# One decoder trunk on one core: compression ahead of d's second pair, other homes for four tiles, and another form of softplus

## Chip, cores and metric

The kernel runs on one core of a Trainium2 chip. The metric is the device time of one execution in microseconds (us); the median of three runs stands for the kernel.

## The reference, cut to what matters

Two layers over 512 tokens of width 1024. In each layer four attention branches read the same normalised input h, each result is gated, projected and merged:

```python
for l in range(DEPTH):                      # DEPTH = 2
    h = rmsnorm(x, norm_g[l])
    c = split_columns(h @ w_in[l])          # columns a_*, b_*, c_*, d_*
    y_a = dilated_window_attention(...) * silu(c["a_gate"])
    y_b = mla_attention(...)            * silu(c["b_gate"])
    y_c = nsa_attention(...)            * silu(c["c_gate"])   # uses compress_blocks
    y_d = stick_breaking_attention(...) * silu(c["d_gate"])
    for i, y in enumerate((y_a, y_b, y_c, y_d)):
        merged += sigmoid(h @ w_merge[l, i] + b_merge[l, i]) * (y @ w_branch[l, i])
    x = x + merged @ w_out[l]
```

Branch d (stick breaking) needs softplus(z) = log(1 + exp(z)) of its scores z, summed from the right, and exp(z - that sum). Compression (`compress_blocks`, for c's first part) takes overlapping blocks of 32 tokens of two 64-wide columns, adds a position table, multiplies by w1 (2048 x 128 for each of the two), applies gelu and multiplies by w2.

## The kernel before, in words

Every product of 1024-long columns is made in three matmuls of a high and a low half (`mm3`, lines 188 to 190), 128 x 128 by 128 x 512. Such a product of one 128-column chunk of weights with all tokens is a **chunk**: its weights come by DMA on the queue of SyncE (SP) into one of 3 `stage` buffers (line 239), ScalarE (L182), GpSimd (L100) and VectorE (L184) split them into halves (4 `w5` tiles, so two chunks), and TensorE runs 24 matmuls (`proj_T`). A chunk of `merge_chunks` has 6 more for the branch (`pd<-y,w`). Chunks need only h (and a y in the merge), so they are the filler between the small matmuls of attention.

An attention pair (two heads) runs the steps scores on TensorE (`qk_unit`, L290, into one of 2 `pss` banks), softmax on VectorE and ScalarE (L300 to L307), transposes (L325, `pt`), a copy on ScalarE (L327) and the product with v (L331, into the one bank `po`). `pv_cluster` holds the last three. Each layer has 30 clusters (6 in b, 6 in a, 6 in d, 12 in c). Branch order is b, a, d, c. In d the scores z go to `ze[0]` (L740), then L742 takes min(z, 30) on VectorE into `ze[1]`, L743 its exponential, L746 log(1 + that) on ScalarE, and L748 takes the larger of z and that on VectorE; prefix sums (L756), a difference (L757) and an exponential (L758) follow. `after(...)` on line 751 orders L748 of two tiles behind the splits of two later weight chunks.

A scheduler orders the instructions of each engine: it takes what is ready by priority, which is the place in the program. `tc.high_priority(offset)` moves a block ahead by `offset` places; the four attention branches are moved ahead of the chunks that stand beside them in the program. Each engine then executes its list in order; a DMA queue too.

Tiles share slots by tag: `s4` has 11, `x4` 4, `y4` 8, PSUM `pd` 3. A new tile waits until a slot is free. Names in what follows:

- b's stage: chunks for b's gate, d's q and k (both pairs) and a's gate, beside b's attention, whose q and k tiles are `x4`.
- a's stage: the two table tiles `tab_a` (`x4`, line 692), a's q and k (`y4`), merge (0, 1), d's gate, then `compress()`, then merge (1, 0).
- `compress()`: chunk c_kc, 8 additions on VectorE (L609) that form the blocks, a chunk for ks and kw (split at L175 and L176 into two `s4` tiles), four w1 tiles of 512 KB (`s4`, DMA of line 626), 16 small matmuls for each (L629).
- d's `ze` tiles are `x4` (four for a pair) and unit tiles.

The functions that the diff touches, with the line numbers of the profile:

Of the kernel before, what the change touches and what calls it, by code (L numbers as in the profile page):

```python
# [12 lines left out]
AF = mybir.ActivationFunctionType  # L13
OP = mybir.AluOpType
PSUM = bass.MemoryType.PSUM

P = 128
# [28 lines left out]
W_SHARE = 5  # L46

PV_GROUPS = ((0, 1), (2,), (3,))
N_S4, N_W5, N_TH, N_PT, N_SU, N_S2 = 11, 4, 2, 4, 5, 4

MERGE_REST = ((2, 0), (2, 1), (2, 3), (3, 0), (3, 3), (0, 3), (3, 1), (1, 3), (0, 2), (1, 2), (2, 2), (3, 2))
# [35 lines left out]
def hybrid_trunk(ctx: ExitStack, tc: tile.TileContext, x, norm_g, w_in, mla_q_norm, mla_w_uq, mla_kv_norm,  # L87
                 mla_w_ukv, nsa_pos, nsa_w1, nsa_b1, nsa_w2, nsa_b2, w_branch, w_merge, b_merge, w_out,
                 final_norm_g, tab_a_d, mask_tab_d, dist_tab_d, cmp_tab_d, rope_tab_d, small_d, out):
    nc = tc.nc  # L90
    V, A, G, T = nc.vector, nc.scalar, nc.gpsimd, nc.tensor
# [16 lines left out]
    def s4(shape, dt=F32):  # L108
        return mk(sb, shape, dt, "s4", N_S4)
# [4 lines left out]
    def x4(shape, dt=F32):  # L114
        return mk(sb, shape, dt, "x4", 4)
# [22 lines left out]
    def ps_d():  # L138
        return mk(ps, [P, 512], F32, "pd", 3)
# [170 lines left out]
    def after(first, then, why):  # L310

        tc.add_manual_dep(then.ins, first.ins.name, mybir.DependencyInfo(
            mybir.DependencyClass.Sync, mybir.DependencyReason.DATA), reason=why)

    def pv_cluster(units, acc):

        blocks = [(u, kb) for u in units for kb in range(u[1] + 1)]
        n = len(blocks)  # L320
        pTs = []
        for h in range(2):
            pt = ps_t().rearrange("p (a q) -> p a q", a=4)
            for i, (u, kb) in enumerate(blocks):
                T.transpose(pt[:, i], u[0][h][:, kb * P:(kb + 1) * P], ident)  # L325
            pT = pt_tile()
            ready = A.activation(pT[:, :n], pt[:, :n], AF.Copy)  # L327
            pTs.append(pT)
        for i, ((_, qt, v, started, last), kb) in enumerate(blocks):
            for h in range(2):  # L330
                pv = T.matmul(acc[64 * h:64 * h + 64, qt * P:(qt + 1) * P], v(h, kb), pTs[h][:, i],  # L331
                              start=(kb == 0 and not started), stop=(kb == qt and last), skip_group_check=True)
                if kb == 0:
                    after(ready, pv, "both heads together")

    def finish_pair(acc, g, y, c):

# [73 lines left out]
    for t in range(NT):  # L411
        x_in.append(x4([P, D]))
        for c0 in range(0, D, 512 if t == 0 else D):
            c = slice(c0, c0 + (512 if t == 0 else D))
# [28 lines left out]
    for l in range(DEPTH):  # L443
# [140 lines left out]
        def compress():  # L584
            b1 = tiny([P, 2], "b1", 1)
            nc.sync.dma_start(b1, nsa_b1[l].rearrange("s p -> p s"))
            b2k = tiny([P, 1], "b2k", 1)
            for hf in range(2):
                nc.sync.dma_start(b2k[64 * hf:64 * hf + 64], nsa_b2[l, 0].rearrange("(d o) -> d o", o=1))
            b2v = tiny([P, 64], "b2v", 1)  # L590
            nc.sync.dma_start(b2v, bcast_rows(nsa_b2[l, 1], 64))
            w2k = tiny([P, 2, 64], "w2k", 1)
            w2v = tiny([P, 64], "w2v", 1)
            for hf in range(2):
                nc.sync.dma_start(w2k[:, hf], nsa_w2[l, 0])
            nc.sync.dma_start(w2v, nsa_w2[l, 1])

            acc = ps_d()
            proj_T(in_chunk(l, COL["c_kc"]), acc)
            blocks = []  # L600
            for s_ in range(2):
                sm = s2([P, 16, 32])
                V.memset(sm[:, :, NCMP:], 0.0)
                tokv = acc[64 * s_:64 * s_ + 64].rearrange("p (n q r) -> p r q n", r=2, q=8)
                for r in range(2):
                    for qh in range(2):
                        src = tokv[:, r, :, qh:qh + NCMP]
                        pos = posT[l][64 * r:64 * r + 64, 16 * s_ + 8 * qh:16 * s_ + 8 * qh + 8, None]
                        V.tensor_tensor(sm[64 * r:64 * r + 64, 8 * qh:8 * qh + 8, :NCMP], src,  # L609
                                        pos.to_broadcast([64, 8, NCMP]), op=OP.add)  # L610
                blocks.append(sm)
            acc = ps_d()
            proj_T(split_chunk([(0, KD, 0, 64, wview(w_in[l], 0, D, COL["c_ks"], 64)),
                                (0, KD, 64, 128, wview(w_in[l], 0, D, COL["c_kw"], 64))], KD), acc)
            ks, kw = s4([P, 2, S], F32R), s4([P, 2, S], F32R)
            for j, o in ((0, ks), (1, kw)):
                src = acc[64 * j:64 * j + 64]
                split(o[:64, 0], o[:64, 1], src)
                for z in range(2):
                    pool_copy(o[64:, z], o[:64, z])  # L620
            hid = tiny([P, 2, 32], "hid", 1)
            acc = ps_d()
            for s_ in range(2):
                for hf in range(2):
                    w1 = s4([P, 8, P])
                    nc.sync.dma_start(w1, nsa_w1[l, s_, 1024 * hf:1024 * hf + 1024].rearrange("(q p) c -> p q c", p=P))
                    for q in range(8 * hf, 8 * hf + 8):
                        g = 32 * (q % 4)
                        T.matmul(acc[g:g + 32, s_ * P:(s_ + 1) * P], blocks[s_][:, q], w1[:, q % 8], start=q < 4,  # L629
                                 stop=q >= 12, skip_group_check=True)  # L630
            gs = s2([P, 2, P])
            A.activation(gs, acc[:, :2 * P].rearrange("p (s c) -> p s c", s=2), AF.Copy)
            pt = ps_t()
            for s_ in range(2):
                T.matmul(pt[:, 32 * s_:32 * s_ + 32], gs[:, s_], sel, start=True, stop=True)
                V.tensor_scalar(hid[:, s_], pt[:, 32 * s_:32 * s_ + 32], b1[:, s_:s_ + 1], None, op0=OP.add)
            c0 = math.sqrt(2.0 / math.pi)
            u = tiny([P, 64], "gelu", 1)
            hf_ = hid.rearrange("p s n -> p (s n)")
            V.tensor_tensor(u, hf_, hf_, op=OP.mult)  # L640
            V.tensor_scalar(u, u, 0.044715, 1.0, op0=OP.mult, op1=OP.add)
            V.tensor_tensor(u, u, hf_, op=OP.mult)
            A.activation(u, u, AF.Tanh, scale=c0)
            V.tensor_scalar(u, u, 0.5, 0.5, op0=OP.mult, op1=OP.add)
            V.tensor_tensor(hf_, u, hf_, op=OP.mult)
            pt = ps_t()
            T.matmul(pt[:, :32], w2k.rearrange("p a d -> p (a d)"), hid[:, 0], start=True, stop=True)
            kc = tiny([P, 32], "kc", 1)
            V.tensor_scalar(kc, pt[:, :32], b2k, None, op0=OP.add)
            hv4 = tiny([P, NH, 32], "hv4", 1)  # L650
            V.tensor_copy(hv4, hid[:, 1][:, None, :].to_broadcast([P, NH, 32]))
            pt = ps_t()
            T.matmul(pt[:, :64], hv4.rearrange("p h n -> p (h n)"), w2v, start=True, stop=True)
            vbd = tiny([P, 2, P], "vbd", 1)
            V.memset(vbd, 0.0)
            for h in range(NH):
                V.tensor_tensor(vbd[32 * h:32 * h + 32, h // 2, 64 * (h % 2):64 * (h % 2) + 64],
                                pt[32 * h:32 * h + 32, :64], b2v[32 * h:32 * h + 32], op=OP.add)
            return ks, kw, kc, vbd
# [3 lines left out]
        a_q, a_k, d_q, d_k = [], [], [], []  # L663
        am, mT = {}, {}
        gb = gate_chunks("b_gate")
        for c in range(2):
            d_q.append(q_chunk("d_q", c, 0.125))
            d_k.append(k_chunk("d_k", c))
        ga = gate_chunks("a_gate")
        with tc.high_priority(offset=tc.cur_priority - mark):  # L670
            y[1] = new_y()
# [33 lines left out]
                finish_pair(acc, ga, y[0], pr)  # L705
        mark = tc.cur_priority
        merge_chunks(l, ((0, 1),), y, am, mT)
        gd = gate_chunks("d_gate")
        ks, kw, kc, vbd = compress()
        n_10 = len(w_split)  # L710
        merge_chunks(l, ((1, 0),), y, am, mT)
        c_q = [q_chunk("c_q", c, cscale[:, c:c + 1]) for c in range(2)]
# [13 lines left out]
        with tc.high_priority(offset=tc.cur_priority - mark):  # L726
            y[3] = new_y()
            for pr in range(2):
# [10 lines left out]
                        s = qk_unit(stacked(d_q[pr], d_k[pr][h], h), qt, w)  # L739
                        V.tensor_tensor(part(0, qt, h), s[:, :w], mask_tab[:, S + 1 - w:], op=OP.subtract)  # L740
                for j in range(3):
                    V.tensor_scalar(ze[1][j], ze[0][j], 30.0, None, op0=OP.min)  # L742
                    ex = A.activation(ze[1][j], ze[1][j], AF.Exp)  # L743
                with tc.issue_after(ex.ins):
                    for j in range(3):
                        A.activation(ze[1][j], ze[1][j], AF.Ln, bias=1.0)  # L746
                for j in range(3):
                    larger = V.tensor_tensor(ze[1][j], ze[0][j], ze[1][j], op=OP.max)  # L748
                    if j < 2:

                        after(w_split[(n_10 + 2, n_11 + 3)[pr] + j], larger, "weights first")
                    for qt in range(NT):
                        if place[qt][0] == j:
                            for h in range(2):
                                er = part(1, qt, h)[:, ::-1]
                                V.tensor_tensor_scan(er, er, er, 0.0, op0=OP.add, op1=OP.bypass)  # L756
                    V.tensor_tensor(ze[0][j], ze[0][j], ze[1][j], op=OP.subtract)  # L757
                    A.activation(ze[0][j], ze[0][j], AF.Exp)  # L758
# [136 lines left out]
```

## Time and profile before

| what | value |
|---|---|
| median of 3 runs | 1097.37 us (1095.41 to 1098.2) |
| profiled execution, its own time | 1094.31 us |
| its span, first to last instruction | 1092.5 us (1.8 us lie around it) |
| TensorE matmul busy (PE) | 1071.1 us, 98% of the span |
| weight load (PEld) | 859.1 us, 79% |
| VectorE (DVE) | 589.0 us, 54% |
| ScalarE (ACT) | 441.8 us, 40% |
| GpSimd (POOL) | 247.9 us, 23% |
| mean granted TensorE clock | 0.995 of full speed |

How to read it: a row `203.80:222.70 18.90, 13.74 (x110) ...` is a stretch of the span in us, its length, and the busy time of each engine in it. PEclk is the granted TensorE clock, 1.00 being 2.4 GHz and 0.50 being 1.2 GHz. In waits, `PE pss L290 <- DVE stat L300` means that TensorE stood before a matmul of line 290 into `pss` until VectorE's line 300 was done; in a timeline the idle time before an instruction stands in brackets. SPq is SyncE issuing DMAs.

### The profile page before, as it was taken

The page shows a single profiled execution, that of the slowest core. Times are in us where ns is not written, and L with a number is a line of the kernel's source. Part 1 is how long each engine was busy: PE and PEld are TensorE (multiplying, and loading weights), DVE is VectorE, ACT ScalarE, POOL GpSimd, SP SyncE. Part 2 cuts the span into 40 slices and gives each one's busy share as a digit, 9 for nine tenths or more (in the row PEclk, how much of TensorE's full clock was granted, in tenths as well). Part 3 has the DMA queues.
Part 4 walks back from the last instruction along what each step waited for, and adds up shares of the span by engine and source line. Part 5 has one row for each costly group of instructions (what it writes and reads, how often), then busy time and mean ns, then how long its engine had stood idle before and what let it go on. Part 6 is the DMA issues. An engine that isn't in the chain of part 4 may idle for free.

```text
span 1092.5 us, 15146 instructions
## 1 busy us (share of the span) xinstructions
PE 1071.1 (98%) x5652; PEld 859.1 (79%) x5652; DVE 589.0 (54%) x1136; ACT 441.8 (40%) x894; POOL 247.9 (23%) x270
## 2 busy tenths in 40 slices
PE   8999999899999999999999999998999999999997
PEld 6888787678788878888888887876878787878886
DVE  6436565755845556345343565457846564643432
ACT  5424444444533434234243344446353343432322
POOL 3231120011213132342011311111022221234321
PEclk9999999989999999999999999999999999999999
DMA  8423242253232221436313333234323322233412
GB/s 249 104 58 78 67 117 68 64 142 90 73 97 73 73 73 49 135 89 190 114 39 98 78 77 87 78 88 130 93 73 97 86 59 73 73 94 94 135 59 78
DMA packets 161676, 100.86 MB, mean 92 GB/s; under 512 B 14913, under 2 KB 151489, under 8 KB 161602
## 3 DMA queue, kind: packets, MB, share of 16 engines
q1 hardware_dynamic: 160880, 98.75, 31.5%
q10 hardware_dynamic: 722, 1.14, 0.3%
q8 instruction: 45, 0.74, 0.3%
q14 instruction: 29, 0.24, 0.1%
HBM read 95.67 MB, written 4.19 MB: 91 GB/s over the span
## 4 chain that ended last, share of the span: by engine, by line
PE 88%; DVE 4%; DMA 4%; ACT 2%; issue 1%; SPq 0%; POOL 0%; POOLq 0%; DVEq 0%; ACTq 0%
PE pd L190 24%; PE pd L188 24%; PE pd L189 24%; PE po L331 5%; PE pt L325 4%; PE pss L290 4%; DMA stage<-in_w_out_dram 3%; DVE w L184 1%; DMA s<-in_nsa_w_dram 1%; DVE su L300 1%; DVE s L609 0%; DMA x<-in_x_dram 0%; PE pt L678 0%; PE pd L629 0%; PE po L189 0%
## 5 line engine op out<-in xcount | busy, mean ns | idle before, releaser
L188 PE MATMUL pd<-hT,w 128*128 128x512 f32 x832 | 333.8, 401 | 0.2
L190 PE MATMUL pd<-hT,w 128*128 128x512 f32 x832 | 332.5, 400 | 0.8 <-DVE w L184 0.7
L189 PE MATMUL pd<-hT,w 128*128 128x512 f32 x832 | 332.5, 400 | 0.0
L100 POOL TENSOR_SCALAR w<-stage 128x640 fp32r<-128x640 f32 (+1 forms) x104 | 71.3, 686 | 619.6 <-PE pd L189 292.8
L190 PEld LDWEIGHTS pd<-hT,w 128*128 128x128 f32 x832 | 157.0, 189 | 37.4 <-DVE w L184 2.5
L188 PEld LDWEIGHTS pd<-hT,w 128*128 128x128 f32 x832 | 157.1, 189 | 36.2 <-issue 1.3
L189 PEld LDWEIGHTS pd<-hT,w 128*128 128x128 f32 x832 | 157.1, 189 | 34.7 <-issue 1.1
L184 DVE TENSOR_TENSOR w<-stage,w 128x1280 fp32r<-128x1280 f32 (+1 forms) x104 | 145.4, 1398 | 66.9 <-ACT w L182 49.6
L182 ACT ACTIVATE w<-stage 128x640 fp32r<-128x640 f32 x104 | 76.4, 737 | 108.1 <-PE pd L189 97.2
L395 POOL TENSOR_TENSOR s<-s,th 128x512 f32<-128x512 f32 x48 | 107.6, 2241 | 44.1 <-DVE th L394 39.8
L327 ACT ACTIVATE pt<-pt 128x384 f32<-128x384 f32 (+2 forms) x120 | 59.4, 521 | 103.4 <-PE pt L325 103.0
L302 ACT ACTIVATE su<-su,stat 128x128 f32<-128x128 f32 (+3 forms) x128 | 71.0, 556 | 53.2 <-DVE stat L300 52.8
L394 DVE SCALAR_TENSOR_TENSOR th<-th,pd 128x512 f32<-128x512 f32 x48 | 32.9, 685 | 99.5 <-PE pd L190 99.5
L387 ACT ACTIVATE th<-pd,bmT 128x512 f32<-128x512 f32 x64 | 43.8, 684 | 88.5 <-PE pd L190 88.4
L325 PE MATMUL pt<-small,su 128*128 128x128 f32 x336 | 57.6, 279 | 1.2 <-DVE su L305 0.7
L189 PE MATMUL pd<-y,w 128*128 128x512 f32 x128 | 50.7, 396 | 0.0
L190 PE MATMUL pd<-y,w 128*128 128x512 f32 x128 | 50.6, 396 | 0.0
L325 PEld LDWEIGHTS pt<-small,su 128*128 128x128 f32 x336 | 39.6, 140 | 13.7 <-issue 6.0
L188 PE MATMUL pd<-y,w 128*128 128x512 f32 x128 | 50.4, 396 | 0.0
L300 DVE CUSTOM_DVE_ANT_0 su<-pss,dist_tab 128x128 f32<-128x128 f32 (+3 forms) x64 | 29.0, 486 | 35.1 <-PE pss L290 35.1
L290 PE MATMUL pss<-s,s 128*128 128x512 f32 (+3 forms) x192 | 44.0, 340 | 2.8 <-DVE su L740 2.0
L189 PE MATMUL pd<-y,hT 128*128 128x512 f32 (+1 forms) x112 | 44.1, 397 | 0.0
(249 smaller groups left out, 1534.4 us busy)
## 6 DMA issues: line engine op xcount, KB each, us to landing
stage<-in_w_merge_dram SPq DMA_DIRECT2D x64, 512.0 KB, 3.9
stage<-in_w_in_dram SPq DMA_DIRECT2D x38, 512.0 KB, 3.9
stage<-in_w_branch_dram SPq DMA_DIRECT2D x64, 128.0 KB, 3.8
stage<-in_w_out_dram SPq DMA_DIRECT2D x16, 512.0 KB, 4.0
stage<-in_w_in_dram SPq DMA_DIRECT2D x20, 256.0 KB, 3.9
s<-in_nsa_w_dram SPq DMA_DIRECT2D x8, 512.0 KB, 4.8
stage<-in_w_in_dram SPq DMA_DIRECT2D x8, 352.0 KB, 4.2
x<-in_tab_a_dram SPq DMA_DIRECT2D x4, 512.0 KB, 6.1
```

The lines of the kernel that those rows point to most:

```text
L100: G.tensor_scalar(o, i, 1.0, 1.0, op0=OP.mult, op1=OP.mult)
L182: A.activation(hi[:, :a], src[:, :a], AF.Copy)
L184: return V.tensor_tensor(lo, src, hi.bitcast(F32), op=OP.subtract)
L188: T.matmul(acc, sh, mh, start=start, stop=False)
L189: T.matmul(acc, sh, ml, start=False, stop=False)
L190: T.matmul(acc, sl, mh, start=False, stop=stop)
L290: T.matmul(s[:, :width], q[:, qt * P:(qt + 1) * P], k[:, :width], start=i == 0, stop=i == len(passes) - 1)
L302: A.activation(e[:, :width], e[:, :width], AF.Exp, scale=-1.0, bias=st[:, 0:1], accum_out=st[:, 1:2])
L325: T.transpose(pt[:, i], u[0][h][:, kb * P:(kb + 1) * P], ident)
L327: ready = A.activation(pT[:, :n], pt[:, :n], AF.Copy)
L331: pv = T.matmul(acc[64 * h:64 * h + 64, qt * P:(qt + 1) * P], v(h, kb), pTs[h][:, i], start=(kb == 0 and not started), stop=(kb == qt and ...
L395: G.tensor_tensor(acc[:, j], acc[:, j], th, op=OP.add)
```

## The change

1. Compression (`compress()`) stays behind merge (0, 1), but d's gate, which stood before it, moves to b's stage, and d's second pair (`d_q[1]`, `d_k[1]`) moves from b's stage to behind compression; `d_k[1]` takes `y4` tiles instead of `s4`.
2. The w1 tiles become `x4` instead of `s4`; the loads of the first two stand ahead of compression's first chunk, those of the last two where they were.
3. The matmuls on w1 (L629) and all products with v (L331) are moved ahead by 4000 places of priority.
4. In d, min(z, 30) on VectorE becomes |z| on ScalarE; the exponential takes -|z|; and instead of the larger of two, VectorE makes max(z, 0) + log(1 + exp(-|z|)) in one instruction.

```diff
@@ -46,6 +46,8 @@
 W_SHARE = 5
 
 PV_GROUPS = ((0, 1), (2,), (3,))
+
+ABOVE = 4000
 N_S4, N_W5, N_TH, N_PT, N_SU, N_S2 = 11, 4, 2, 4, 5, 4
 
 MERGE_REST = ((2, 0), (2, 1), (2, 3), (3, 0), (3, 3), (0, 3), (3, 1), (1, 3), (0, 2), (1, 2), (2, 2), (3, 2))
@@ -326,12 +328,13 @@
             pT = pt_tile()
             ready = A.activation(pT[:, :n], pt[:, :n], AF.Copy)
             pTs.append(pT)
-        for i, ((_, qt, v, started, last), kb) in enumerate(blocks):
-            for h in range(2):
-                pv = T.matmul(acc[64 * h:64 * h + 64, qt * P:(qt + 1) * P], v(h, kb), pTs[h][:, i],
-                              start=(kb == 0 and not started), stop=(kb == qt and last), skip_group_check=True)
-                if kb == 0:
-                    after(ready, pv, "both heads together")
+        with tc.high_priority(offset=ABOVE):
+            for i, ((_, qt, v, started, last), kb) in enumerate(blocks):
+                for h in range(2):
+                    pv = T.matmul(acc[64 * h:64 * h + 64, qt * P:(qt + 1) * P], v(h, kb), pTs[h][:, i],
+                                  start=(kb == 0 and not started), stop=(kb == qt and last), skip_group_check=True)
+                    if kb == 0:
+                        after(ready, pv, "both heads together")
 
     def finish_pair(acc, g, y, c):
 
@@ -595,6 +598,12 @@
                 nc.sync.dma_start(w2k[:, hf], nsa_w2[l, 0])
             nc.sync.dma_start(w2v, nsa_w2[l, 1])
 
+            def w1_load(s_, hf):
+                w1 = x4([P, 8, P])
+                nc.sync.dma_start(w1, nsa_w1[l, s_, 1024 * hf:1024 * hf + 1024].rearrange("(q p) c -> p q c", p=P))
+                return w1
+
+            w1s = [w1_load(0, 0), w1_load(0, 1)]
             acc = ps_d()
             proj_T(in_chunk(l, COL["c_kc"]), acc)
             blocks = []
@@ -622,12 +631,12 @@
             acc = ps_d()
             for s_ in range(2):
                 for hf in range(2):
-                    w1 = s4([P, 8, P])
-                    nc.sync.dma_start(w1, nsa_w1[l, s_, 1024 * hf:1024 * hf + 1024].rearrange("(q p) c -> p q c", p=P))
-                    for q in range(8 * hf, 8 * hf + 8):
-                        g = 32 * (q % 4)
-                        T.matmul(acc[g:g + 32, s_ * P:(s_ + 1) * P], blocks[s_][:, q], w1[:, q % 8], start=q < 4,
-                                 stop=q >= 12, skip_group_check=True)
+                    w1 = w1s[hf] if s_ == 0 else w1_load(s_, hf)
+                    with tc.high_priority(offset=ABOVE):
+                        for q in range(8 * hf, 8 * hf + 8):
+                            g = 32 * (q % 4)
+                            T.matmul(acc[g:g + 32, s_ * P:(s_ + 1) * P], blocks[s_][:, q], w1[:, q % 8],
+                                     start=q < 4, stop=q >= 12, skip_group_check=True)
             gs = s2([P, 2, P])
             A.activation(gs, acc[:, :2 * P].rearrange("p (s c) -> p s c", s=2), AF.Copy)
             pt = ps_t()
@@ -663,9 +672,9 @@
         a_q, a_k, d_q, d_k = [], [], [], []
         am, mT = {}, {}
         gb = gate_chunks("b_gate")
-        for c in range(2):
-            d_q.append(q_chunk("d_q", c, 0.125))
-            d_k.append(k_chunk("d_k", c))
+        d_q.append(q_chunk("d_q", 0, 0.125))
+        d_k.append(k_chunk("d_k", 0))
+        gd = gate_chunks("d_gate")
         ga = gate_chunks("a_gate")
         with tc.high_priority(offset=tc.cur_priority - mark):
             y[1] = new_y()
@@ -705,8 +714,9 @@
                 finish_pair(acc, ga, y[0], pr)
         mark = tc.cur_priority
         merge_chunks(l, ((0, 1),), y, am, mT)
-        gd = gate_chunks("d_gate")
         ks, kw, kc, vbd = compress()
+        d_q.append(q_chunk("d_q", 1, 0.125))
+        d_k.append(k_chunk("d_k", 1, y4))
         n_10 = len(w_split)
         merge_chunks(l, ((1, 0),), y, am, mT)
         c_q = [q_chunk("c_q", c, cscale[:, c:c + 1]) for c in range(2)]
@@ -739,13 +749,13 @@
                         s = qk_unit(stacked(d_q[pr], d_k[pr][h], h), qt, w)
                         V.tensor_tensor(part(0, qt, h), s[:, :w], mask_tab[:, S + 1 - w:], op=OP.subtract)
                 for j in range(3):
-                    V.tensor_scalar(ze[1][j], ze[0][j], 30.0, None, op0=OP.min)
-                    ex = A.activation(ze[1][j], ze[1][j], AF.Exp)
+                    A.activation(ze[1][j], ze[0][j], AF.Abs)
+                    ex = A.activation(ze[1][j], ze[1][j], AF.Exp, scale=-1.0)
                 with tc.issue_after(ex.ins):
                     for j in range(3):
                         A.activation(ze[1][j], ze[1][j], AF.Ln, bias=1.0)
                 for j in range(3):
-                    larger = V.tensor_tensor(ze[1][j], ze[0][j], ze[1][j], op=OP.max)
+                    larger = V.scalar_tensor_tensor(ze[1][j], ze[0][j], 0.0, ze[1][j], op0=OP.max, op1=OP.add)
                     if j < 2:
 
                         after(w_split[(n_10 + 2, n_11 + 3)[pr] + j], larger, "weights first")
```

## Rows read from the trace of the kernel before

**Rows 1.** The page, busy time of an engine, share of the span, instructions.

```profile
PE 1071.1 (98%) x5652; PEld 859.1 (79%) x5652; DVE 589.0 (54%) x1136; ACT 441.8 (40%) x894; POOL 247.9 (23%) x270
```

**Rows 2.** Windows: length, busy time by engine, clock, DMA share and rate.

```profile
203.80:222.70 18.90, 13.74 (x110) 9.83 (x109) 15.26 (x45) 14.24 (x30) 3.89 (x5) 0.95 0.40 114
222.70:227.80 5.10, 5.10 (x16) 4.05 (x13) 2.66 (x4) 3.44 (x5) 0.00 (x0) 0.51 0.90 247
741.60:759.50 17.90, 13.31 (x110) 9.32 (x108) 15.51 (x45) 12.84 (x28) 3.89 (x5) 1.00 0.40 115
```

**Rows 3.** Waits of TensorE, whole span: total us, times, longest.

```profile
PE pd L629 <- DMA s<-in_nsa_w_dram: 3.1, 2, 2.1
...
PE pss L290 <- DVE stat L300: 2.6, 2, 1.3
PE pss L290 <- DVE su L740: 2.0, 2, 1.1
...
PE pt L325 <- DVE su L305: 0.7, 2, 0.3
PE pss L290 <- DVE x L740: 0.6, 2, 0.5
...
PE pt L325 <- ACT pt L327: 0.5, 1, 0.5
```

**Rows 4.** Timeline of TensorE, first w1 matmuls of each layer.

```profile
221.66 1.08 PE L629 MATMUL pd<-s,s 128*32 128x128 f32 x16 [2.07 <-DMA s<-in_nsa_w_dram]
...
758.84 0.65 PE L629 MATMUL pd<-s,s 128*32 128x128 f32 x16 [1.07 <-DMA s<-in_nsa_w_dram]
```

**Rows 5.** Timeline of SP's queue in the first layer, a's stage.

```profile
156.03 0.81 SPq L692 DMA_DIRECT2D x<-in_tab_a_dram  x2
...
217.54 5.63 SPq L626 DMA_DIRECT2D s<-in_nsa_w_dram  x4
```

**Rows 6.** Waits of SP's queue, whole span.

```profile
SPq L626 <- PE pss L290: 18.2, 2, 9.5
```

**Rows 7.** Line 626, from issue to landing in us.

```profile
DMA to landing us min/median/max: 4.1/4.8/6.6
```

**Rows 8.** Timeline of VectorE, split of merge (1, 0)'s first weights.

```profile
200.29 1.49 DVE L184 TENSOR_TENSOR w<-stage,w 128x1280 fp32r<-128x1280 f32 x1
```

**Rows 9.** Single lines of d and one of the merge: ns min/median/max.

```profile
L742 DVE TENSOR_SCALAR x<-x x8: 683/694/695, 213.2 to 804.3; 128x1024 f32<-128x1024 f32 x8
L742 DVE TENSOR_SCALAR su<-su x4: 411/420/428, 219.3 to 811.8; 128x512 f32<-128x512 f32 x4
...
L743 ACT ACTIVATE x<-x x8: 1043/1059/1061, 214.0 to 805.1; 128x1024 f32<-128x1024 f32 x8
...
L743 ACT ACTIVATE su<-su x4: 630/632/633, 219.8 to 812.3; 128x512 f32<-128x512 f32 x4
...
L746 ACT ACT_TABLE_LOAD  x4: 1283/1283/1283, 220.4 to 813.0; - x4
...
L748 DVE TENSOR_TENSOR su<-su,su x4: 665/678/693, 224.3 to 818.9; 128x512 f32<-128x512 f32 x4
...
L394 DVE SCALAR_TENSOR_TENSOR th<-th,pd x48: 669/687/689, 264.7 to 1042.8; 128x512 f32<-128x512 f32 x48
```

**Rows 10.** Timeline, two copies of L327 and the products with v behind them.

```profile
194.28 0.60 ACT L327 ACTIVATE pt<-pt 128x512 f32<-128x512 f32 x1 [2.98 <-PE pt L325]
...
199.25 0.44 PE L331 MATMUL po<-pt,s 128*64 128x128 f32 x4
...
214.93 0.58 ACT L327 ACTIVATE pt<-pt 128x512 f32<-128x512 f32 x1
...
215.98 1.09 PE L331 MATMUL po<-pt,s 128*64 128x128 f32 x16
```

**Rows 11.** Timeline, last write of c's result y[2] and its first reader.

```profile
446.46 0.69 DVE L341 TENSOR_TENSOR y<-su,y 128x512 fp32r<-128x512 f32 x1 [0.70 <-ACT y L340]
...
449.48 0.40 PE L188 MATMUL pd<-y,w 128*128 128x512 f32 x1
```

## The prediction

> **What bounds the kernel now.** I read the page first: TensorE is busy 98% of the span [rows 1], so only its idle time and its slow time can be won; its work is the same before and after. Windows of 20 us over the span then showed it full everywhere but at the start, at the end and in one stretch of each layer, and I read those two at their own borders [rows 2]. In layer 1 the stretch lasts 18.90 us and TensorE works 13.74, so 5.16 are idle; in layer 2 it is 17.90 and 13.31, so 4.59. Behind the first stretch the granted clock is 0.51 over 5.10 us, which is its 1.2 GHz level: 5.10 x 0.49 = 2.50 us lost, and the 16 matmuls just ahead took 1.08 instead of the 0.65 of layer 2 [rows 4], 0.43 more. Together 5.16 + 4.59 + 2.50 + 0.43 = 12.7 us: all that the change can reach, short of the ends of the kernel.
>
> The waits say who is late there [rows 3]: the load of w1 (3.1), a's softmax (line 300, 2.6), d's subtraction (line 740, 2.0 and 0.6), a's scaling (line 305, 0.7) and a copy (0.5), together 9.5 of the 9.75 idle us. The stretch is the end of a's second pair and the start of d's first. It has no chunk in it, although merge (1, 0)'s first weights were split at 200.29 + 1.49 = 201.8 us [rows 8]; the first chunk matmul comes only behind the first w1 matmuls, at 222.7. So the reader is to see two faults: w1 late, and no filler while attention waits for VectorE.
>
> Why w1 is late is in SP's queue. Its four loads go out at 217.5 [rows 5], after a wait of up to 9.5 us for score matmuls of line 290 [rows 6]: those read d's q and k, whose `s4` slots w1 needs. Counted in the code, v (2), d's q and k (6), two gates (2) and one accumulator of the merge (1) are all 11 slots, so ks, kw and w1 queue behind d's first scores. Landing takes 4.1 to 6.6 us more [rows 7].
>
> **The change part by part.** *w1 in `x4`.* After b, two of the four slots hold a's tables, issued at 156.0 [rows 5]; two are free, so the first two w1 tiles can be issued then, and even the slowest landing of 6.6 us is over 50 us before the present first use. The last two need a table's slot or that of a used w1 tile. d's `ze` tiles, which need all four, now stand behind w1. I cost the load wait at -3.1 (bounds: nothing gained, if the last two are placed too early, and 3.1); the cover is merge (0, 1) and the two compression chunks. If that cover is gone, 4.8 us a layer are late.
>
> *The order.* Two chunks of d's gate go ahead into b's stage and two of d's second pair come back out of it: each is one chunk and one DMA, so b keeps the number of its chunks, and compression with its fourteen DMAs (seven small ones, three for its chunks, four of w1) passes d's gate on SP. The `s4` count falls to v 2, d 3, gates 2, accumulator 1, ks and kw 2, `d_q[1]` 1, again 11, but with ks, kw and no w1 waiting. Direct cost nothing; the work that hides it is the same number of chunks on both sides. `d_k[1]` in `y4` waits for a's second pair to leave its slots; behind it only its own PSUM bank stands still, and two banks carry on. What comes of this: with w1 past, the chunks of d's second pair and merge (1, 0) lie ready for the empty stretch. Bounds of the other waits (9.75 - 3.1 = 6.6): nothing, if TensorE's list still holds no chunk there, and 6.6, if every wait has one. I take all of it, since 201.8 against 222.7 shows chunks that were ready and unplaced, and with it the clock's 2.9.
>
> *Where that goes next.* Filler used here is missing later. c's result is ready at 446.46 + 0.69 = 447.2 and its first reader starts at 449.5 [rows 11]: only 2.3 us, so in layer 1 chunks run out just as c ends. Three or four chunks used earlier leave c's last clusters bare, except for the chunks whose first 24 matmuls need no y. The price of bare clusters is bounded by nothing and by what a's three bare clusters cost now, 2.6 + 0.7 + 0.5 = 3.8 us over both layers [rows 3]. I take the 3.8, since the rows show the same kind of work there.
>
> *Softplus.* VectorE loses 8 x 0.694 + 4 x 0.420 = 7.2 us and ScalarE gains, at the price of its exponential on the same tiles, 8 x 1.059 + 4 x 0.632 = 11.0. The combined instruction is bounded by the larger-of-two it replaces (0.678 at 512 columns) and the nearest of its own kind (0.687) [rows 9]: nothing. Both hide under TensorE while it has chunks; the scores' buffers come free a little sooner, which is inside the 6.6. I cost it at 0 (bounds: 3.8 of loss, 11.0 - 7.2 all exposed, and a gain no larger than the 2.6 of line 740).
>
> *The Trainium skill on it.* "ScalarE: Activation LUTs", section "Rules for kernel authors", puts simple elementwise work on VectorE and not on ScalarE. The rows agree on the single instruction (0.69 against 1.06), but in the stretch VectorE is the busier one. By that rule the sum would be 5.1 in place of 8.9; the sum here stays with the rows.
>
> *Priority.* The products with v can now start sooner behind their copies. In front of a chunk they start 199.25 - 194.88 = 4.4 us behind, in the bare stretch 215.98 - 215.51 = 0.5 [rows 10]. That 0.5 was enough there for no idle time, so I cost it at 0; bounds 0 and a whole copy of 0.6 for each of 60 clusters, 36 us.
>
> Sum: 12.7 - 3.8 = 8.9 us. The profiled execution took 1094.31, and would take 1085.4. It lies 3.1 under the median of the runs, 1097.37, about their own spread; from the median I get **1088.5**.
>
> **Rivals.**
> A. *ScalarE takes VectorE's place and the stretch stays bare.* For: 14.24 of 18.90 us are already busy on it, 12.84 of 17.90 in layer 2 [rows 2], and 2 x 1.06 + 0.63 = 2.75 come in. Then the stretches shrink only to 16.99 and 15.59, which wins 1.9 + 2.3, and 2.9 more if the clock holds: 4.2 to 7.1, about 1091.7. Against: the chunks that were ready.
> B. *The wait moves to w1's second half.* The last table's slot comes free only with a's last softmax, inside the stretch, and its DMA stands at SP's head until then; with priority 4000 ahead the matmuls stand in TensorE's list at once. Each layer waits up to 4.8: 8.9 - 9.6, so about 1098. For: the same wait shows now. Against: used w1 tiles free slots earlier.
> C. *Slower: products with v stand before their copies.* If all 60 clusters are placed on the copy's heels and half a copy, 0.3 us, is late, 18 us are lost: 1106.5. It decides from 8.9 / 60 = 0.15 us each. For: 4.4 us of room go. Against: the bare stretch, with 0.5 of room, shows no such wait.
> D. *The absolute value brings table loads.* A load is 1.283 us [rows 9]; two for each of 12 tiles would put 30.8 us on ScalarE, up to 1119 if bare. No row has an absolute value. The Trainium skill, "ScalarE: Activation LUTs", section "Table sets: the hidden batching unit", says that it is in every set, so that there would be no load; no run shows that yet.
>
> **How the numbers follow.** Chances: the forecast 0.52 (its own range 1084.5 to 1092.5: from all 12.7 won to 5 of it), A 0.15, B 0.15, C 0.16, D 0.02. 0.3% of the median, about what a measurement of this kernel can tell from no change, is 3.3 us. Faster: nearly all of the forecast, 0.50, most of A, 0.13, and a B that waits for less than half, 0.03: 0.66. Same: the rest of A and B, 0.16. Slower: C and D, 0.18. The range goes from all won, 1084, to 1100.5, past A and B; it leaves out C, D and a sliver below.
>
> **What would show it.** Right: the w1 loads start near 160 and only the late two near the matmuls; chunk matmuls stand between a's last clusters; no wait of line 629 on its DMA; no clock of 0.51 in the first layer; line 742 gone and 12 absolute values of 1.06 and 0.63 on ScalarE, with as many table loads as now; some idle time near c's end. Wrong: a row of line 629 waiting for its DMA again (B); a bare stretch with ScalarE as the one waited for (A); many rows of line 331 waiting for line 327 (C); more table loads (D); or c's end idle for far more than 1.9 us a layer, which would make the term 3.8 the failing one.

## The result, and the profile after

The changed kernel takes **1102.36 us** (median of 5 runs, 1101.65 to 1103.55) against 1095.41 for the kernel before in the same measurement (5 runs, 1094.05 to 1098.2): ratio **1.0063, 95% interval 1.0049 to 1.0077**. It is slower; 1088.5 was forecast, and the time lies above the range. The profiled execution took 1102.45 us, with a span of 1100.6.

First the page of the changed kernel (engine, busy us, share of the span, instructions):

```profile
PE 1072.8 (97%) x5652; PEld 864.2 (79%) x5652; DVE 587.2 (53%) x1124; ACT 454.0 (41%) x910; POOL 245.2 (22%) x270
```

Against [rows 1] the span grew by 8.1 us: TensorE is busy for 1.7 us more, and idle for 27.8 us in place of 21.4. So most of the loss is idle time; work at half clock counts as busy. Now the windows of [rows 2] again, and behind them stretches that were not looked at before (columns as there):

```profile
203.80:222.70 18.90, 18.90 (x101) 15.41 (x100) 13.76 (x32) 8.63 (x21) 2.81 (x3) 1.00 0.24 64
222.70:227.80 5.10, 5.10 (x36) 4.18 (x35) 1.52 (x3) 3.00 (x4) 0.00 (x0) 1.00 0.00 0
233.63:236.90 3.27, 0.00 (x0) 0.00 (x0) 0.85 (x2) 3.24 (x4) 0.44 (x1) 1.00 0.00 0
236.90:243.40 6.50, 3.67 (x10) 3.08 (x11) 4.12 (x9) 5.26 (x7) 0.00 (x0) 0.50 0.07 13
...
741.60:759.50 17.90, 17.90 (x96) 14.66 (x95) 14.10 (x33) 10.51 (x27) 3.82 (x4) 1.00 0.29 81
...
776.30:786.00 9.70, 6.50 (x17) 5.25 (x18) 6.89 (x15) 5.62 (x7) 0.00 (x0) 0.50 0.32 81
```

The reader is to see two things. The stretch that was bare is full: 18.90 of 18.90 and 17.90 of 17.90, where [rows 2] had 13.74 and 13.31, and the clock behind the first one is 1.00 in place of 0.51. And some 10 us later TensorE stands still (0.00 of 3.27 us in the row from 233.63, at a clock still of 1.00), and behind that the clock is 0.50, its 1.2 GHz level, in the rows of 6.50 us and, in layer 2, of 9.70 us.

Who is late there, by the waits of TensorE (us in total, times, longest). Lines of the changed kernel have higher numbers: its 184, 186, 292, 302, 327, 329 and 334 are 182, 184, 290, 300, 325, 327 and 331 of the kernel before.

```profile
PE pt L656 <- issue: 9.4, 2, 4.7
PE pd L190 <- ACT w L184: 2.9, 2, 1.4
...
PE pd L190 <- DVE s L571: 1.8, 2, 1.0
PE pt L327 <- ACT x L768: 1.2, 1, 1.2
PE po L334 <- ACT pt L329: 1.2, 2, 0.6
PE pss L292 <- DVE su L750: 0.8, 2, 0.4
```

Every wait of [rows 3] is gone or small. In their place stand 9.4 us ahead of line 656, the first small product of the compression behind its gelu, and 2.9 for line 184, ScalarE's share of the split of a weight chunk. "issue" says that this view names no releaser for line 656; TensorE's own timeline and ScalarE's, laid side by side, give one. First TensorE:

```profile
233.23 0.40 PE L192 MATMUL pd<-y,w 128*128 128x512 f32 x1
238.31 0.61 PE L656 MATMUL pt<-hid,w2k 128*128 128x32 f32 x2 [4.68 <-issue]
240.34 0.80 PE L190 MATMUL pd<-hT,w 128*128 128x512 f32 x1 [1.43 <-ACT w L184]
```

Then ScalarE over the same time. Line 753 is d's exponential, 756 its logarithm, 652 the tanh of gelu, 768 the exponential behind d's scan:

```profile
232.21 0.63 ACT L753 ACTIVATE su<-su 128x512 f32<-128x512 f32 x1
232.86 1.28 ACT L756 ACT_TABLE_LOAD   x1
234.15 2.00 ACT L756 ACTIVATE x<-x 128x1024 f32<-128x1024 f32 x2
236.17 1.28 ACT L652 ACT_TABLE_LOAD   x1
237.47 0.26 ACT L652 ACTIVATE gelu<-gelu 128x64 f32<-128x64 f32 x1
237.74 1.28 ACT L756 ACT_TABLE_LOAD   x1
239.03 0.63 ACT L756 ACTIVATE su<-su 128x512 f32<-128x512 f32 x1
239.57 1.35 ACT L184 ACTIVATE w<-stage 128x640 fp32r<-128x640 f32 x2
```

ScalarE is never idle for more than 0.02 us here. Merge (1, 0)'s last chunk ends at 233.63. The next two things that TensorE could do both wait for ScalarE: line 656 for a tanh that ends at 237.73, and c's first chunk for its weights, whose split starts at 239.57. Ahead of both stand d's logarithms, and the tanh, placed between the logarithms, brings two table loads more. Layer 2 has the same order, from 771.97 on. The trace has 13 loads of 1283 ns in this kernel and 9 in the one before.

In the kernel before, the same work stood in another place. ScalarE's timeline there (line 746 is the logarithm, 182 the split, 643 the tanh):

```profile
220.41 1.28 ACT L746 ACT_TABLE_LOAD   x1
221.71 2.00 ACT L746 ACTIVATE x<-x 128x1024 f32<-128x1024 f32 x2
223.62 0.61 ACT L746 ACTIVATE su<-su 128x512 f32<-128x512 f32 x1
...
233.70 0.74 ACT L182 ACTIVATE w<-stage 128x640 fp32r<-128x640 f32 x1 [0.52 <-PE pd L189]
...
244.31 0.26 ACT L643 ACTIVATE gelu<-gelu 128x64 f32<-128x64 f32 x1 [1.77 <-DVE gelu L642]
```

The logarithms were done at 224.23, while merge (1, 0)'s chunks, which start at 222.68, still had work for TensorE, and the next split and the tanh came behind them, one after the other.

The Trainium skill, "ScalarE: Activation LUTs", section "What ACT_TABLE_LOAD costs", adds 1.38 us of drain to a load. No row here shows it: the load at 232.86 ends at 234.14 and the logarithm starts at 234.15.

### The profile page after: what moved, and what is told of

Same layout as the page of the kernel before. It is cut to its first block, busy times and chain, and to the rows that moved or that the text cites. A ratio compares the mean times of both kernels' runs of the same rounds, so it can differ in the third digit from the quotient of the medians.

```text
span 1100.6 us, 15136 instructions
## 1 busy us (share of the span) xinstructions
PE 1072.8 (97%) x5652; PEld 864.2 (79%) x5652; DVE 587.2 (53%) x1124; ACT 454.0 (41%) x910; POOL 245.2 (22%) x270
## 4 chain that ended last, share of the span: by engine, by line
PE 88%; DVE 4%; ACT 3%; DMA 2%; issue 1%; SPq 0%; POOL 0%; POOLq 0%; DVEq 0%; ACTq 0%
PE pd L190 24%; PE pd L191 24%; PE pd L192 23%; PE po L334 5%; PE pss L292 5%; PE pt L327 4%; DMA stage<-in_w_out_dram 2%; DVE x L766 1%; DVE w L186 1%; PE pt L687 1%; ACT L756 0%; ACT x L756 0%; DMA stage<-in_w_in_dram 0%; ACT w L184 0%; PE pss L228 0%
## 5 line engine op out<-in xcount | busy, mean ns | idle before, releaser
L102 POOL TENSOR_SCALAR w<-stage 128x640 fp32r<-128x640 f32 (+1 forms) x104 | 76.5, 737 | 650.3 <-PE pd L191 316.3
L398 POOL TENSOR_TENSOR s<-s,th 128x512 f32<-128x512 f32 x48 | 101.5, 2114 | 37.7 <-DVE th L397 31.9
L327 PE MATMUL pt<-small,su 128*128 128x128 f32 x336 | 57.8, 278 | 0.0
L327 PEld LDWEIGHTS pt<-small,su 128*128 128x128 f32 x336 | 40.3, 140 | 13.8 <-issue 6.1
L191 PE MATMUL pd<-y,hT 128*128 128x512 f32 (+1 forms) x112 | 44.0, 396 | 0.0
L190 PE MATMUL pd<-y,hT 128*128 128x512 f32 (+1 forms) x112 | 43.4, 397 | 0.0
L192 PE MATMUL pd<-y,hT 128*128 128x512 f32 (+1 forms) x112 | 43.4, 392 | 0.0
```

Source lines behind the costliest of these rows:

```text
L102: G.tensor_scalar(o, i, 1.0, 1.0, op0=OP.mult, op1=OP.mult)
L190: T.matmul(acc, sh, mh, start=start, stop=False)
L191: T.matmul(acc, sh, ml, start=False, stop=False)
L192: T.matmul(acc, sl, mh, start=False, stop=stop)
L398: G.tensor_tensor(acc[:, j], acc[:, j], th, op=OP.add)
```

## The experiments

Theories, as the expectations name them. **J**: the new loss is ScalarE's order at d's first softplus, gelu's tanh with two loads between the logarithms and c's weight split behind them. **F**: chunks are used earlier and are missing later, whoever is late then. **S**: the absolute value on ScalarE costs time. **P**: products with v stand before their copies. Twelve runs of eleven kernels were made ("both ahead" twice), on several chips; ratios are to the kernel before on the same chip, with their 95% interval.

**1. Without the tanh.** The changed kernel, with gelu's tanh left out, so that it computes something else:

```diff
-            A.activation(u, u, AF.Tanh, scale=c0)
```

> The changed kernel without gelu's tanh (that one function is left out of the compressed values, so they differ from the reference's); with it go two table loads of 1.283 us a layer. J (the stall sits in ScalarE's order at d's first softplus: tanh and its two loads between the logarithms, and c's weight split behind them): the 4.68 us in front of w2k's matmul is gone, the split comes some 2.8 us earlier, 1093 to 1098. F (the chunks were simply used up earlier, whatever ScalarE does): no change, 1100 to 1103. S (the absolute value on ScalarE costs it): no change, 1100 to 1103.

1094.03 us, ratio 1.000 (0.999 to 1.0009). Nine table loads again, the wait of line 656 is gone, and TensorE waits 2.7 us a layer for line 184. J's number; the ratio falls by 0.63%, about 7 us, for one instruction of 0.26 a layer and the two loads that come with it.

**2 to 4. Nothing left out, only ScalarE's order.** `after(x, y, why)` puts y behind x in the list of its engine:

```diff
-                    for j in range(3):
-                        A.activation(ze[1][j], ze[1][j], AF.Ln, bias=1.0)
+                    lns = [A.activation(ze[1][j], ze[1][j], AF.Ln, bias=1.0) for j in range(3)]
+                    if pr == 0:
+                        for ln in lns:
+                            after(gelu_tanh[-1], ln, "gelu first")
```

This is "both ahead". "Behind" has `after(ln, gelu_tanh[-1], "logarithms first")` as its last line; "split ahead" has that too and, before it, `after(hi_split[m_10 + 2], ln, "weights of c first")`. The lists `gelu_tanh` and `hi_split` hold gelu's tanh and ScalarE's parts of the splits; number `m_10 + 2` is the part for c's first chunk.

"Behind" puts the tanh behind all three logarithms; "split ahead" also puts the split of c's first chunk ahead of them; "both ahead" asks only for the tanh ahead of them, and the split then lands ahead of them too.

> The changed kernel with gelu's tanh ordered behind all three logarithms of d's first pair: nine table loads in place of thirteen, all work kept; c's weight split still stands behind the logarithms. J: two loads and the wait before w2k's matmul gone, TensorE still idle about 4 us until the split: 1093 to 1098. F and S: 1100 to 1103.

> As the run with tanh behind the logarithms, and ScalarE's part of the split of c's first weight chunk ordered ahead of them. J: TensorE has that chunk as soon as VectorE has made its low half, about 1.7 us after merge (1, 0) ends, and the clock holds: 1087 to 1092. F: little change against the changed kernel, 1099 to 1103, as there is no chunk to be had. S: 1099 to 1103.

> The changed kernel with gelu's tanh ordered ahead of the three logarithms of d's first pair; the order on ScalarE then has tanh, the split of c's first weight chunk, one table load, the logarithms. J: as with the split ahead, 1087 to 1092. F: 1099 to 1103. S: 1099 to 1103.

> The repaired kernel (gelu's tanh ahead of d's first logarithms) once more, beside its twin with the old softplus. J: 1088 to 1091, a ratio of 0.994 to 0.997 to the kernel before. If the earlier gain was luck of one chip: above 0.998.

| kernel | median us | ratio to before |
|---|---|---|
| tanh behind | 1096.74 | 1.0019 (1.0006 to 1.0031) |
| split ahead | 1093.44 | 0.9992 (0.9979 to 1.0006) |
| both ahead | 1089.48 | 0.9959 (0.9944 to 0.9973) |
| both ahead, once more | **1088.62** | **0.9938 (0.9925 to 0.9951)** |

With the tanh behind, the two extra loads are gone and line 184 is the wait:

```profile
PE pd L190 <- ACT w L184: 9.9, 4, 3.7
```

With both ahead (second run), ScalarE's timeline reads (line 755 is the logarithm here):

```profile
230.66 0.63 ACT L753 ACTIVATE su<-su 128x512 f32<-128x512 f32 x1
231.22 0.26 ACT L652 ACTIVATE gelu<-gelu 128x64 f32<-128x64 f32 x1
231.47 0.74 ACT L184 ACTIVATE w<-stage 128x640 fp32r<-128x640 f32 x1
232.22 1.28 ACT L755 ACT_TABLE_LOAD   x1
233.52 2.01 ACT L755 ACTIVATE x<-x 128x1024 f32<-128x1024 f32 x2
```

The tanh follows the exponential without a load, which agrees with the Trainium skill, "ScalarE: Activation LUTs", section "Table sets: the hidden batching unit", where both are in one set. What stays is a wait of 1.35 us a layer for VectorE's share of the split:

```profile
PE pd L192 <- DVE w L186: 3.3, 3, 1.4
```

J's times held but for "split ahead", 1.4 us above its band. There the same wait is 7.6 us over six times; why VectorE's share comes later than with both ahead was not followed. The last ratio, 0.9938, is just below the 0.994 that J gave. "Both ahead" beats both kernels.

**5, 6. Softplus alone, and everything but softplus.** The kernel before with the new softplus, and the changed kernel with the old one:

```diff
-                    V.tensor_scalar(ze[1][j], ze[0][j], 30.0, None, op0=OP.min)
-                    ex = A.activation(ze[1][j], ze[1][j], AF.Exp)
+                    A.activation(ze[1][j], ze[0][j], AF.Abs)
+                    ex = A.activation(ze[1][j], ze[1][j], AF.Exp, scale=-1.0)
```

In both, the larger-of-two goes with it: max and add in the first kernel, larger-of-two again in the second.

> The kernel before with the new softplus alone (absolute value on ScalarE, max and add in one instruction). J: 11 us more on ScalarE and 7 less on VectorE, hidden, but the table loads may move: within 0.4% of before. S: this is what costs, 6 to 8 us more than before.

> The changed kernel with the old softplus (min on VectorE, exponential, larger of two). Tanh still stands between logarithms and there are two table loads more than in the changed kernel. J: the stall stays, 1099 to 1104. S: the loss is gone, about 1088.

Alone 1096.49, ratio 1.0027 (1.0012 to 1.0042); undone 1101.88, 1.0075 (1.0046 to 1.0103), against the changed kernel's 1.0063. The repaired kernel "both ahead" was also run with the old softplus:

> The repaired kernel with the old softplus (minimum and larger-of-two on VectorE). My sum, softplus at 0: within 2 us of the repaired kernel on the same chip, 1087.5 to 1091.5. S, the absolute value costs ScalarE time that is bare (the skill's rule, simple work on VectorE): 1085 to 1087.5. Rival, VectorE is the late one in the stretch and the new form is what keeps it from waiting: 1091.5 to 1095, with new waits of d's subtraction or of the scaling behind it.

1090.15, 0.9949 (0.9934 to 0.9963), where its twin on the same chip has 0.9938 (0.9925 to 0.9951). So the new softplus costs 0.27% alone and saves 1.5 us in the repaired kernel (by the medians; the two intervals overlap): it depends on what stands around it. S falls as the cause of the changed kernel's loss, which stays with the old softplus. Alone the new softplus has 13 table loads too: there, in d's second pair, the tanh of a gate (line 567) stands between the logarithms, at 283.69 and 822.76.

**7, 8. The order alone, and w1 alone.** The kernel before with the new order of chunks only (`gd` ahead, `compress()` ahead of `d_q[1]` and `d_k[1]`), and with w1 in `x4`, loaded early and with priority, only:

> The kernel before with the new order of chunks alone (d's gate in b, d's second pair behind compression); w1 in its old slots, old softplus, no priority. Tanh stands behind the logarithms here. J: no stall at w2k's matmul, w1 still late or less late: 1090 to 1097. F (moving chunks ahead of d's softplus is what costs): 1099 or more.

> The kernel before with w1 in the table tiles, loaded early, and its matmuls with priority; chunk order, softplus and the products with v as before. J, the new stall comes of the new order, which brings gelu's tanh among d's logarithms: no stall of the kind here, nine table loads, the 3.1 us of the w1 wait gone and some of the other waits, 1089 to 1094. F, chunks used earlier are missing later whatever the order: 1096 or more.

Order 1102.79, ratio 1.0085 (1.006 to 1.0111); w1 1100.36, 1.0047 (1.0031 to 1.0062). J missed both, F hit the number of both. In the first, though, the place is not d's softplus: the largest wait of TensorE is that for a's softmax of [rows 3], grown from 2.6, with all four of its waits in a's attention (197.0 and 199.1 in layer 1, 737.8 and 739.2 in layer 2). With the same 5652 matmuls TensorE is also busy for 1080.1 us, 9.0 more than before; why was not followed.

```profile
PE pss L290 <- DVE stat L300: 6.7, 4, 2.4
```

With w1 alone the stall of the changed kernel is there with the old order and the old softplus. TensorE, then ScalarE (line 753 is the logarithm, 183 the split, 650 the tanh here):

```profile
233.29 0.39 PE L191 MATMUL pd<-y,w 128*128 128x512 f32 x1
237.43 0.69 PE L189 MATMUL pd<-hT,w 128*128 128x512 f32 x1 [3.75 <-ACT w L183]
237.91 0.63 PE L190 MATMUL pd<-hT,w 128*128 128x512 f32 x1
240.14 0.80 PE L189 MATMUL pd<-hT,w 128*128 128x512 f32 x1 [1.60 <-ACT w L183]
```

```profile
233.46 1.28 ACT L753 ACT_TABLE_LOAD   x1
234.75 2.00 ACT L753 ACTIVATE x<-x 128x1024 f32<-128x1024 f32 x2
236.66 0.72 ACT L183 ACTIVATE w<-stage 128x640 fp32r<-128x640 f32 x1
...
237.92 1.28 ACT L650 ACT_TABLE_LOAD   x1
239.21 0.26 ACT L650 ACTIVATE gelu<-gelu 128x64 f32<-128x64 f32 x1
239.37 0.72 ACT L183 ACTIVATE w<-stage 128x640 fp32r<-128x640 f32 x1
```

So J is too narrow. The chunks run out here as soon as w1 is early, as F has it, and the next chunk's weights stand behind d's logarithms whether a tanh is among them or behind them all ("tanh behind", 3.7); a tanh among them makes it longer.

**9, 10. Priority.** The changed kernel with `ABOVE = 0`, and with the priority kept for w1's matmuls but not for the products with v (theories G and W are in the expectation; the second edit is shown):

```diff
-        with tc.high_priority(offset=ABOVE):
+        with tc.high_priority(offset=0):
             for i, ((_, qt, v, started, last), kb) in enumerate(blocks):
```

> The changed kernel without the 4000 places of priority for the products with v and the matmuls on w1. J: tanh still stands between logarithms, 1098 to 1104. P (the products with v stand before their copies and cost the time): about 1088.

> The changed kernel with the priority kept for w1's matmuls and taken from the products with v. G, the priority's worth is that it keeps the products with v in 60 groups: the groups break up into about 110, each break costs 0.2 us and the way back 0.2 to 0.26, so 1111 to 1119 as with no priority at all. W, w1's own priority was what mattered: 1100 to 1104.

No priority 1116.85, ratio 1.0213 (1.0188 to 1.0239), further off than either theory had it; products with v plain 1122.52, 1.0247 (1.0233 to 1.0262), beyond G's band and far from W's. In the first, where w1 has no priority either, TensorE does not wait before line 656, but 4.7 us for line 186 and 4.6 for line 660; in the second it waits 9.3 before line 656, as in the changed kernel (9.4). TensorE is busy for 1092.6 us in the last one, 19.8 more than with the priority, with the same 5652 matmuls. Windows over the whole span, for the 800 products with v alone (us, busy TensorE and weight load, clock, DMA), first the changed kernel, then the plain one:

```profile
0.00:1121.00 1121.00, 56.92 (x800) 42.44 (x800) 0.99 0.31 90
```

```profile
0.00:1121.00 1121.00, 73.31 (x800) 46.51 (x800) 0.99 0.31 90
```

Where that comes from, in one cluster of d: the changed kernel's timeline, then the plain one's.

```profile
262.44 1.09 PE L334 MATMUL po<-pt,s 128*64 128x128 f32 x16
263.46 0.55 PE L327 MATMUL pt<-small,x 128*128 128x128 f32 x3
```

```profile
263.10 0.66 PE L334 MATMUL po<-pt,s 128*64 128x128 f32 x8
263.69 0.33 PE L327 MATMUL pt<-small,x 128*128 128x128 f32 x1
263.95 0.43 PE L334 MATMUL po<-pt,s 128*64 128x128 f32 x2
264.31 0.33 PE L327 MATMUL pt<-small,x 128*128 128x128 f32 x1
264.57 0.43 PE L334 MATMUL po<-pt,s 128*64 128x128 f32 x2
264.93 0.33 PE L327 MATMUL pt<-small,x 128*128 128x128 f32 x1
265.19 0.44 PE L334 MATMUL po<-pt,s 128*64 128x128 f32 x4
```

Sixteen products and three transposes take 1.57 us from first start to last end in two groups, and 2.53 with the products in four, both at a granted clock of 1.00: 0.32 us for each further group. Over the trace the products stand in 60 groups with the priority and in 111 without, and 51 x 0.32 = 16 of the 20 us, an estimate from this one cluster; the 800 products alone are busy for 16.4 us more. Neither J nor P had priced that.

## Why the prediction was wrong, step by step

- **w1 in `x4`: right.** Its first two loads go out at 158.34, the others at 184.22 and 192.49, its first matmuls run at 191.8, and none waits for its DMA. B did not happen.
- **The empty stretch: right in size.** All 12.7 us came: both stretches are full and the first clock of 0.51 is gone.
- **"Where that goes next": the step that failed, place and size.** It looked for the missing chunks at c's end [rows 11] and priced them at 3.8 us. At c's end TensorE waits for nothing. They are missing at d's first softplus, right behind the stretch: by the waits above 9.4 + 2.9 there, 0.8 + 1.2 near it (lines 750 and 768 as releasers) and 1.8 at d's second pair, some 60 us on (line 571), 16.1 us of idle time, and 3.67 + 6.50 us of work at half clock, 5.1 lost. So the term of 3.8 came to 21.2. 12.7 won and 21.2 lost make 8.5 slower; the spans of the two profiles differ by 8.1, the medians by 7.0. In the kernel before, merge (1, 0)'s chunks, from 222.7 on, had covered d's logarithms.
- **"Direct cost nothing; the work that hides it is the same number of chunks on both sides": wrong.** The count was right, the count was not what mattered. A chunk hides a wait only if its weights are split, and a part of each split is queued on ScalarE, in order, here behind the very work that was to be hidden (the split at 239.57 behind the logarithm at 239.03). Alone the order costs 0.85%, but by another stall, a's softmax at 6.7; that d's gate, which left a's stage, had covered it is argued, not shown.
- **Softplus at 0: right within about 3 us.** A fails in its place: the stretch did not stay bare. But its thought, that ScalarE becomes the late engine, is what happened 10 us later, by its order and not by the 2.75 us of absolute values: with the old softplus the kernel is as slow.
- **Priority at 0: its effect was not seen.** It was only weighed as a risk (C, 0.3 us in each cluster). The products wait 1.2 us in all for their copies, and in this kernel the priority saves 20 us by keeping them together. The kernel before has 60 groups without it, so this is no gain over before; it prevents a loss that the other edits would have brought. Which of them breaks the groups up stays open: with w1 alone there are 64, with the order alone 65.
- **D: did not happen.** No absolute value has a load ahead of it; 8 take 1058 ns and 4 take 624. The Trainium skill ("ScalarE: Activation LUTs", section "Table sets: the hidden batching unit") has it in every set; the trace agrees in all 12 places. The four extra loads belong to the tanh.

That the failing step is this one, and not the 12.7, the repair shows: with the tanh ordered ahead on ScalarE, which brings one split along, and no other edit, the kernel takes 1088.62 and 1089.48. That this meets the forecast of 1088.5 is in part chance, as the kernel before was faster there than the 1097.37 of the forecast: by the ratios the repair wins 6.8 and 4.5 us of the forecast 8.9. Even so repaired, the second run has 8.4 us of new waits (lines 186, 571, 329, 770, 750 and 184 as releasers), none of them at c's end. ScalarE's order is thus shown as the cause of most of the stall. That w1's part (other slots, early loads, priority) by itself uses the chunks up is shown by its kernel with the order and softplus of before. Not followed is how the three parts, 0.27%, 0.47% and 0.85% slower alone, share the loss of the whole: they don't add up, 1.6% against 0.63%.

## What to carry to other kernels

When a change fills a hole with work that was ready, ask what that work had been covering, and walk the timeline forward to the next place with no other cover; here it was 10 us away, not 220. Count filler as ready only when every engine that prepares it has an instruction free of the work to be covered, and read each in-order queue there from the top. Where two functions of different tables share ScalarE, write their order down: one tanh of 0.26 us in the wrong place made two loads a layer and most of this loss (a ratio of 1.0063, and 1.0019 with the tanh behind).

## What the runs showed of the hardware

- Products with 64 columns and transposes with 128 that alternate cost 0.32 us for each further group in the cluster shown, at full clock. With 111 groups in place of 60 TensorE is busy for 19.8 us longer without one more matmul.
- The clock fell to 1.2 GHz in and behind each of the two idle times of 4.68 us in the changed kernel (236.9 and 776.3). With 1.35 us of idle time at the same place, in the repaired kernel, the second layer kept 1.00 and the first had 0.79 over six us:

```profile
236.00:242.00 6.00, 6.00 (x24) 4.90 (x23) 5.93 (x7) 1.36 (x4) 0.65 (x1) 0.79 0.63 179
...
770.00:776.00 6.00, 6.00 (x30) 4.92 (x29) 5.89 (x8) 2.88 (x5) 0.94 (x1) 1.00 0.64 181
```

- The combined instruction on VectorE takes 1220 ns at 1024 columns and 678 at 512, the same as the larger-of-two that it replaces (1222 and 678).
